# Where the small steps of a hybrid decoder layer stand between its projections: yields moved, and 6 + 10 attention tiles in place of 8 + 8

## The chip, the cores and the metric

The kernel runs on one core of one Trainium2 chip. The metric is the device time of one execution in microseconds (us). The kernel before took 2392.32 us, the median of 3 runs (2391.59 to 2392.73).

Engines: TensorE (PE; PEld is its weight load) does matmuls, VectorE (DVE) and ScalarE (ACT) work element by element and also read PSUM, GpSimd (POOL) works on SBUF, SyncE (SP) issues nearly all DMAs, one after the other.

## The reference

Two layers over one sequence of 256 positions with 2048 channels. Each layer:

```python
mod = c_act @ ada_w + ada_b                 # shift, scale, gate (2048 each)
h = rmsnorm(x, norm_w) * (1 + scale) + shift
u = h @ w_in                                # all projections in one
# branch A: gated DeltaNet, 16 heads of 128: causal conv (4 taps) + SiLU on q, k, v,
#   L2-normed q and k, decay g = -exp(a_log) * softplus(a + dt), chunked delta rule
#   (a unit lower-triangular solve in each chunk), RMSNorm per head, times SiLU(z_A)
# branch B: sliding-window (128) attention, 32 query and 4 key/value heads of 64,
#   rotary positions, a learned sink per head, times SiLU(z_B)
y = sigmoid(g_a) * (o_a @ proj_a) + sigmoid(g_b) * (o_b @ proj_b)
x = x + gate * (y @ w_out)
```

and a final RMSNorm. Everything is float32.

## The kernel before, in words

**Projections.** Activations stand transposed: 128 channels on the partitions, 256 positions along the free dimension. All weight matrices are cut into tiles of 128 output channels. `_plan` (line 46) writes out the order of the 181 tiles of a layer; the main loop (from line 946) takes them one by one. A tile is one *projection*: 16 steps over the 2048 input channels, each of two matmuls (`mm_k`, lines 291 and 292), because weights and activations are split in a high and a low part. Weights come from HBM in two halves of 512 KB (`load_half`): SP loads `win`, ScalarE casts the high part `whi` (line 203), VectorE forms the low part `wlo` (line 204). The rings: 5 `win`, 4 `whi`, 3 `wlo`. A projection's result lies in one of 2 PSUM buffers `mm` until `evac` (lines 318 and 319: ScalarE copies one half, VectorE adds the other) has put it into one of 3 buffers `ub`. The first 32 tiles of layer 0 and 8 of layer 1 are done in another way, ahead of the loop.

**Order in a layer.** After those come ba (beta and decay), kb and vb (keys and values of attention), and then two batches. A batch has 8 heads of branch A: qa 8 times, va 8 times, ka 8 times, and then 8 attention tiles, each a query and a gate projection (qb, zb) for a pair of heads. In batch 1 the second kb and vb stand between va and ka. Attention tiles 0 to 7 use the first kb and vb, 8 to 15 the second (`j = t // 8`, line 821). Then za (16), pa (16), pb (16) and wo (16), with the ga and gb that are left.

**What is done between projections.** After a projection's matmuls the loop calls `advance()`, then `run_bg(1)`, then the tile's handler. Handlers are generators: what stands behind `yield w` is issued `w` projections later than the next one's `advance()`. So `yield 0` means: behind the matmuls of the next projection; `yield 1`: behind those of the one after it. This is the order in which instructions are written; the framework then schedules them by expected readiness, with this order as priority, so an instruction may stand later than it was written, in the middle of a projection.
- `h_qa`, `h_va`, `h_ka`: convolution and SiLU of one head (`conv_silu`, from line 510: one multiply on ScalarE, three steps on VectorE at line 516, SiLU at 517). After every second head a pair is transposed on TensorE (`sumsq`, line 523, tile `sst`, with sums of squares on ScalarE at line 529; for va the transposes at line 713, tile `vtr`, scaled into `bV` at line 716).
- `h_ba`: transposes of beta and decay (`bat`), softplus as some 25 small steps on VectorE, prefix sums on TensorE (`gcp`, lines 492 and 493), a transpose (`gcr`) and a store.
- `gdn_e`: at the batch's first qa, loads the decays into `E` (1 MB broadcast), subtracts 16 times on VectorE (line 559) and takes the exponential on ScalarE (561).
- `gdn` (a background generator; every projection takes it to its next `yield`): norms, Gram matrices (`gram`, lines 613 and 614), a triangular inverse of 32-blocks in 31 small double steps on VectorE (lines 637 and 639, in five segments), a round trip through HBM, the inverse put together on TensorE (`T1p`, `Y1p`, `T2p`, `Y2p`), and the chunk steps `r`, `s1`, `ks`, `o0`, `r`, `o1`, sums of squares of the output, its norm. It begins with the last pair of ka and has 27 steps.
- `h_zb`: scores (`sc`, line 826) after the next projection, softmax on VectorE and ScalarE, transposes (`ptr`) two projections later, values (`pv`) two after those.
- `h_za` for head 8 and on needs batch 1's `gdn` to be finished: a loop runs what is left of it at once.
- Layer 0 also carries *ada* work, the modulations of gate and of layer 1: rows of 1 MB are loaded in halves into the `win` ring and multiplied and summed on VectorE (line 170). `ADA_RATE` says how many rows per projection: in layer 0 0.45 in qa and ka, 0.35 in va, 0.1 in qb and zb, 0.54 in za; in layer 1 none in these stages.

**Buffers that matter.** One buffer each: `E` (later `LX`, in which the inverse is made), `ek` (`eg` and `kdec`), `qT`, `kT`, `bV`, `GT`, `QKT`, `Y`, the rotated keys `kr`, the attention values `vnat`, the rotated query. Three: `vT` and `ub`. Two: `rot`. PSUM besides `mm`: 6 buffers for all small matmuls.

Of the kernel before, what the change touches and what calls it, by code (L numbers as in the profile page):

```python
# [25 lines left out]
HB = 8  # L26
# [19 lines left out]
def _plan(l):  # L46
    p = [("ga", i) for i in range(min(GRP[l], 16))] + [("gb", i) for i in range(GRP[l] - 16)]
    p += [("ba", 0), ("kb", 0), ("vb", 0)]
    for b in range(NB):
        for what in ("qa", "va", "ka"):  # L50
            p += [(what, b * HB + h) for h in range(HB)]
            if b == 1 and what == "va":
                p += [("kb", 1), ("vb", 1)]
        for t in range(8 * b, 8 * b + 8):
            p += [("qb", t), ("zb", t)]
    p += [("za", h) for h in range(NH)]
    for i in range(16):
        if i >= GRP[l]:
            p.append(("ga", i))
        p.append(("pa", i))  # L60
    for i in range(16):
        if i >= GRP[l] - 16:
            p.append(("gb", i))
        p.append(("pb", i))
    p += [("wo", i) for i in range(16)]
    return p
# [53 lines left out]
def build(nc):  # L120
# [11 lines left out]
    with ExitStack() as ctx:  # L132
# [26 lines left out]
        def big(name, shape, tag, dt=F32):  # L159
            return b8.tile(shape, dt, name=name, tag=tag, bufs=2 if tag == "oT" else 1)  # L160

        def gps(name, shape):
            return psg.tile(shape, F32, name=name, tag="g")
# [152 lines left out]
        def evac(ps):  # L316
            t = sm.tile([P, S], F32, name="ub", tag="ub", bufs=3)
            A.copy(t, ps[:, S:2 * S])  # L318
            V.tensor_tensor(t, t, ps[:, 0:S], op=ALU.add)  # L319
            return t  # L320
# [97 lines left out]
        for l in range(L):  # L418
# [24 lines left out]
            def cols_to_rows(cols_ap, n, name):  # L443
                pt = gps(name + "_t", [n, P])
                T.transpose(pt, cols_ap, ident)
                s = sm.tile([n, P], F32, name=name + "_s", tag="rowt", bufs=1)
                A.copy(s, pt)
                return s
# [11 lines left out]

            def h_ba(ps, i):
                u = evac(ps)
                pt = gps("bat", [P, 2, 64])
                for m in range(2):
                    T.transpose(pt[:, m, 0:48], u[0:48, m * P:(m + 1) * P], ident[0:48, 0:48])
                A.activation(beta, pt[:, :, 0:16], AF.Sigmoid)
                z = sm.tile([P, 2, NH], F32, name="spz", tag="spz", bufs=1)
                V.tensor_tensor(z, pt[:, :, 32:48],
                                pr[:, PC_DT:PC_DT + 16].unsqueeze(1).broadcast_to([P, 2, NH]), op=ALU.add)
                e = sm.tile([P, 2, NH], F32, name="spe", tag="spe", bufs=1)  # L470
                A.activation(e, z, AF.Abs)
                A.activation(e, e, AF.Exp, scale=-1.0)
                s = sm.tile([P, 2, NH], F32, name="sps", tag="sps", bufs=1)
                V.tensor_scalar(s, e, 2.0, None, op0=ALU.add)
                V.reciprocal(s, s)
                V.tensor_tensor(s, s, e, op=ALU.mult)
                s2 = sm.tile([P, 2, NH], F32, name="sps2", tag="sps2", bufs=1)
                V.tensor_tensor(s2, s, s, op=ALU.mult)
                q = sm.tile([P, 2, NH], F32, name="spq", tag="spq", bufs=1)
                V.memset(q, 1.0 / 17)  # L480
                for c in (15, 13, 11, 9, 7, 5, 3, 1):
                    V.tensor_tensor(q, q, s2, op=ALU.mult)
                    V.tensor_scalar(q, q, 1.0 / c, None, op0=ALU.add)
                V.scalar_tensor_tensor(q, q, 2.0, s, op0=ALU.mult, op1=ALU.mult)
                V.tensor_scalar(z, z, 0.0, None, op0=ALU.max)
                V.tensor_tensor(q, q, z, op=ALU.add)
                na = sm.tile([P, NH], F32, name="nega", tag="nega", bufs=1)
                A.activation(na, pr[:, PC_ALOG:PC_ALOG + 16], AF.Exp)
                V.tensor_scalar(na, na, -1.0, None, op0=ALU.mult)
                V.tensor_tensor(q, q, na.unsqueeze(1).broadcast_to([P, 2, NH]), op=ALU.mult)  # L490
                pg = gps("gcp", [P, 3, NH])
                T.matmul(pg[:, 0:2, :], tri, q, start=True, stop=True)
                T.matmul(pg[:, 2, :], ones, q[:, 0, :], start=True, stop=True)
                V.tensor_copy(gc, pg[:, 0:2, :])
                V.tensor_tensor(edec, pg[:, 2, :], gc[:, 0, :], op=ALU.subtract)
                A.activation(edec, edec, AF.Exp)
                A.activation(egc1, gc[:, 1, :], AF.Exp)
                s = cols_to_rows(gc.rearrange("p m h -> p (m h)"), 2 * NH, "gcr")
                for m in range(2):
                    dma(gc_dram[:, m, :], s[m * NH:(m + 1) * NH, :])  # L500
# [34 lines left out]
            def h_qa(ps, i):  # L535
                b, hh = divmod(i, HB)
                g = batch(b)
                if hh == 0:
                    gdn_e(b)
                    g["qT"] = big("qT", [P, HB, S], "qT")  # L540
                conv_silu(ps, i, g["qT"][:, hh, :])
                if hh % 2 == 1:
                    yield 0
                    sumsq(g["qT"], g["ssq"], hh - 1)

            def gdn_e(b):
# [16 lines left out]
            def h_ka(ps, i):  # L563
                b, hh = divmod(i, HB)
                g = batch(b)
                if hh == 0:
                    g["kT"] = big("kT", [P, HB, S], "kT")
                conv_silu(ps, 16 + i, g["kT"][:, hh, :])
                if hh % 2 == 1:
                    yield 0  # L570
                    sumsq(g["kT"], g["ssk"], hh - 1, g["kdec"])
                    if hh == HB - 1:
                        bg.append(gdn(b))

            def gdn(b):
                yield from gdn_k(b)
                yield from gdn_core(b)

            def gdn_k(b):
# [29 lines left out]
                for hh in range(HB):  # L609
                    p = gps("gram", [P, 2, 2, P])  # L610
                    for m in range(2):
                        kk = kT[:, hh, m * P:(m + 1) * P]
                        T.matmul(p[:, 0, m, :], kk, kk, start=True, stop=True)
                        T.matmul(p[:, 1, m, :], kk, qT[:, hh, m * P:(m + 1) * P], start=True, stop=True)
                    V.tensor_tensor(GT[:, hh], GT[:, hh], p[:, 0], op=ALU.mult)
                    V.tensor_tensor(QKT[:, hh], E[:, hh], p[:, 1], op=ALU.mult)
                    if hh % 3 == 2 or hh == HB - 1:
                        yield 1
                gdr = drp.tile([2 * HB, 4, 32, 32], F32, name="gdr", tag="gdr")
                for blk in range(4):  # L620
# [34 lines left out]
                for blk in range(4):  # L655
                    r = slice(32 * blk, 32 * blk + 32)
                    dma(Y[r, :, r], ydr[:, blk].rearrange("q j i -> j q i"))
                    if blk < 3:
                        d = Xa[r, :, r] if blk < 2 else Xb[r]
                        dma(d, xdr[:, blk].rearrange("q j i -> j q i"))  # L660
                yield 1
                yield 1
                GTv = GT.rearrange("p h m t -> p (h m) t")
# [34 lines left out]
            def h_va(ps, i):  # L698
                b, hh = divmod(i, HB)
                g = batch(b)  # L700
                if hh == 0:
                    g["bV"] = big("bV", [P, HB, 2, P], "bV")
                vT = sm.tile([P, S], F32, name="vT", tag="tA", bufs=3)
                conv_silu(ps, 32 + i, vT)
                if hh % 2 == 0:
                    g["vT"] = vT
                    return
                pair = (g["vT"], vT)
                yield 0
                p = gps("vtr", [P, 2, 2, P])  # L710
                for e in range(2):
                    for m in range(2):
                        T.transpose(p[:, e, m, :], pair[e][:, m * P:(m + 1) * P], ident)
                for e in range(2):
                    for m in range(2):
                        A.mul(g["bV"][:, hh - 1 + e, m, :], p[:, e, m, :], beta[:, m, i - 1 + e:i + e])

            def gdn_core(b):
# [32 lines left out]
                for h0 in range(0, HB, 4):  # L751
                    sumsq(oT, g["sso"], h0)
                    sumsq(oT, g["sso"], h0 + 2)
                    yield 1
                sso = g["sso"]
                V.tensor_scalar(g["ssq"], g["ssq"], P * EPS, P * EPS * EPS, op0=ALU.mult, op1=ALU.add)
                V.scalar_tensor_tensor(sso, sso, 1.0 / P, g["ssq"], op0=ALU.mult, op1=ALU.add)
# [305 lines left out]
```

## Time and profile before

| | |
|---|---|
| runs, median | 2392.32 us |
| the profiled execution | 2387.45 us, span of the core 2385.7 us |
| mean granted TensorE clock | 0.994 |
| busy: PE, PEld, DVE, ACT, POOL | 2298.6, 2018.0, 1792.3, 1434.1, 119.9 us |
| the loop's projections | layer 0 from 218.0 us, layer 1 from 1275.3 us |

Rows of the views have these forms. *Waits*: an engine and line, what it waited for, us in total, times, longest. *Windows*: from and to, length, busy us of PE, PEld, DVE, ACT, POOL (with instruction counts), granted clock, DMA share, GB/s. *Groups*: line, engine, operation, out<-in, shapes, count, busy us, mean ns, idle time before it and what ended it. *Timeline*: start, duration, engine, line, operation, and in brackets the idle time before it. TensorE's matmuls are pipelined: their durations overlap.

### The profile page before, as it was taken

How to read it: one execution, taken by the hardware profiler on the slowest of the kernel's cores; microseconds unless marked ns; L12 is line 12 of the kernel's file. 1: busy time of each engine (PE TensorE's matmuls, PEld its weight loads, DVE VectorE, ACT ScalarE, POOL GpSimd, SP SyncE). 2: the span in 40 equal slices, each digit the busy share in tenths (PEclk: the TensorE clock that was granted, in tenths of full speed). 3: DMA queues.
4: the chain of work that ended last, by engine and by line, in shares of the span. 5: the costliest groups of instructions: out<-in, count | busy, mean ns of one | idle time of the engine just before them, and what ended most of it. 6: DMA issues, size and time to landing. Idle time of an engine off the chain costs nothing.

```text
span 2385.7 us, 40190 instructions
## 1 busy us (share of the span) xinstructions
PE 2298.6 (96%) x14838; PEld 2018.0 (85%) x14838; DVE 1792.3 (75%) x3114; ACT 1434.1 (60%) x2691; POOL 119.9 (5%) x128
## 2 busy tenths in 40 slices
PE   7999998999999999999999999999999999999997
PEld 6999787878878887888788888888888888888886
DVE  7998887777787868888676777857678457677766
ACT  4546656777657765444455667778677665444442
POOL 0000000210002100000000001100011000000000
PEclk8999999999999999999999999999999999999999
DMA  9998667566666567999766555555555558777764
GB/s 369 353 362 283 229 227 236 158 195 199 228 234 197 178 218 259 325 308 306 221 196 213 172 182 171 159 178 174 190 169 163 172 180 269 239 244 248 248 202 144
DMA packets 192375, 536.50 MB, mean 225 GB/s; under 512 B 42737, under 2 KB 76593, under 8 KB 186545
## 3 DMA queue, kind: packets, MB, share of 16 engines
q1 hardware_dynamic: 192178, 533.93, 67.3%
q8 instruction: 117, 1.92, 0.3%
q14 instruction: 80, 0.66, 0.1%
HBM read 512.26 MB, written 16.88 MB: 222 GB/s over the span
## 4 chain that ended last, share of the span: by engine, by line
PE 65%; DVE 15%; DMA 11%; ACT 3%; issue 3%; POOL 1%; SPq 1%; DVEq 0%; ACTq 0%; POOLq 0%
PE mm L291 33%; PE mm L292 17%; DVE wlo L204 6%; DMA adaw<-ada 4%; PE mmg L253 2%; PE mmg L251 2%; PE mmg L252 2%; DMA win<-w 2%; DMA xs_dram<-x 2%; DVE LX L639 1%; DVE mt L637 1%; DMA rr<-rr_d 1%; ACT whi L203 1%; DVE cv L516 1%; DVE adaw L170 1%
## 5 line engine op out<-in xcount | busy, mean ns | idle before, releaser
L291 PE MATMUL mm<-h,whi 128*128 128x512 f32 x3616 | 1292.4, 397 | 14.4 <-DVE ub L319 14.1
L204 DVE TENSOR_TENSOR wlo<-win,whi 128x1024 fp32r<-128x1024 f32 x724 | 885.7, 1226 | 300.3 <-PE mm L292 178.5
L292 PE MATMUL mm<-h,wlo 128*128 128x256 f32 x3616 | 1025.6, 284 | 0.0
L203 ACT CAST whi<-win 128x1024 fp32r<-128x1024 f32 x724 | 755.4, 1049 | 407.1 <-PE mm L291 231.0
L291 PEld LDWEIGHTS mm<-h,whi 128*128 128x128 f32 x3616 | 681.0, 188 | 170.6 <-issue 9.2
L292 PEld LDWEIGHTS mm<-h,wlo 128*128 128x128 f32 x3616 | 681.7, 189 | 1.2 <-DVE wlo L204 0.4
L170 DVE SCALAR_TENSOR_TENSOR adaw<-adaw,cact 128x1024 f32<-128x1024 f32 x128 | 155.9, 1225 | 62.1 <-DMA adaw<-ada 61.8
L291 PE MATMUL mm<-yhl,whi 128*128 128x512 f32 x512 | 181.3, 396 | 6.6 <-DVE x L916 4.5
L291 PE MATMUL mm<-oAhl,whi 128*128 128x512 f32 x512 | 181.0, 395 | 2.2 <-DVE oAhl L324 1.8
L291 PE MATMUL mm<-oBhl,whi 128*128 128x512 f32 x512 | 180.7, 396 | 0.0
L319 DVE TENSOR_TENSOR ub<-ub,mm 128x256 f32<-128x256 f32 x290 | 120.8, 417 | 62.2 <-ACT ub L318 61.9
L516 DVE SCALAR_TENSOR_TENSOR cv<-ub,par,cv 128x253 f32<-128x253 f32 (+2 forms) x288 | 137.8, 480 | 33.7 <-ACT cv L514 30.0
L251 PE MATMUL mmg<-h,whi 128*128 128x256 f32 x512 | 140.3, 286 | 9.1 <-ACT h L376 9.1
L292 PE MATMUL mm<-oAhl,wlo 128*128 128x256 f32 x512 | 144.2, 282 | 1.9 <-DVE wlo L204 1.9
L292 PE MATMUL mm<-yhl,wlo 128*128 128x256 f32 x512 | 144.3, 282 | 0.0
L292 PE MATMUL mm<-oBhl,wlo 128*128 128x256 f32 x512 | 144.0, 281 | 0.0
L252 PE MATMUL mmg<-h,whi 128*128 128x256 f32 x512 | 143.5, 287 | 0.0
L253 PE MATMUL mmg<-h,wlo 128*128 128x256 f32 x512 | 137.4, 287 | 2.3 <-DVE wlo L204 2.2
L318 ACT COPY ub<-mm 128x256 f32<-128x256 f32 x290 | 107.1, 369 | 45.9 <-PE mm L292 44.2
L291 PEld LDWEIGHTS mm<-yhl,whi 128*128 128x128 f32 x512 | 96.1, 188 | 31.6 <-issue 7.4
L291 PEld LDWEIGHTS mm<-oAhl,whi 128*128 128x128 f32 x512 | 96.1, 188 | 25.5 <-DVE oAhl L324 2.1
L291 PEld LDWEIGHTS mm<-oBhl,whi 128*128 128x128 f32 x512 | 96.2, 188 | 22.9
(257 smaller groups left out, 2767.0 us busy)
## 6 DMA issues: line engine op xcount, KB each, us to landing
win<-w SPq DMA_DIRECT2D x724, 512.0 KB, 4.9
adaw<-ada SPq DMA_DIRECT2D x128, 512.0 KB, 5.0
adab<-ada SPq DMA_DIRECT2D x32, 1024.0 KB, 8.7
sg<-sig_dram SPq DMA_DIRECT2D x40, 128.0 KB, 2.5
rot<-ub SPq DMA_DIRECT2D x144, 32.0 KB, 2.2
sig_dram<-gacc SPq DMA_DIRECT2D x4, 1024.0 KB
E<-gc_dram SPq DMA_DIRECT2D x4, 1024.0 KB
GT<-GT_d SPq DMA_DIRECT2D x4, 1024.0 KB
```

Of the source, the lines that this page charges most:

```text
L170: V.scalar_tensor_tensor(t, t, 1.0, cact[:, hf * 1024:(hf + 1) * 1024], op0=ALU.mult, op1=ALU.mult, accum_out=acc[:, hf:hf + 1])
L203: A.copy(h, w)
L204: V.tensor_tensor(o, w, h.bitcast(F32), op=ALU.subtract)
L251: T.matmul(d, hi, m[:, 0:S], start=(k == b0 and t % 2 == 0), stop=False)
L252: T.matmul(d, hi, m[:, S:2 * S], start=False, stop=False)
L253: T.matmul(d, lo, m[:, 0:S], start=False, stop=(k == b1 - 1 and t % 2 == 1))
L291: T.matmul(ps[:, :], hi[k // 8][:, c0:c0 + P], m, start=(k == 0), stop=False)
L292: T.matmul(ps[:, S:2 * S], lo[k // 8][:, c0:c0 + P], m[:, 0:S], start=False, stop=(k == KT - 1))
L318: A.copy(t, ps[:, S:2 * S])
L319: V.tensor_tensor(t, t, ps[:, 0:S], op=ALU.add)
L516: V.scalar_tensor_tensor(y[:, j:], u[:, :S - j], w(3 - j), y[:, j:], op0=ALU.mult, op1=ALU.add)
L637: V.tensor_tensor(tv, Xt[:, 0:j + 1, j:j + 1].broadcast_to([64, j + 1, n]), Lt[:, j:j + 1, j + 1:32].broadcast_to([64, j + 1, n]), op=ALU. ...
```

## The change

`_plan` gives batch 0 attention tiles 0 to 5 and batch 1 tiles 6 to 15; the second kb and vb stay where they were, so tiles 6 and 7, which use the first ones, now come behind them. `h_ba` is cut by two more yields and its first transposes come behind one. The pairs of qa, ka and va are transposed one projection later. The background generator takes four Gram heads to a step in place of three (one step less), has four empty steps in place of two behind the inverse's DMAs, and takes the sums of squares of the output in one step in place of two: 27 steps as before. No computation is added or removed.

```diff
-        for t in range(8 * b, 8 * b + 8):
+        for t in (range(0, 6) if b == 0 else range(6, 16)):
             p += [("qb", t), ("zb", t)]
...
             def h_ba(ps, i):
                 u = evac(ps)
+                yield 0
                 pt = gps("bat", [P, 2, 64])
...
                 V.tensor_tensor(q, q, na.unsqueeze(1).broadcast_to([P, 2, NH]), op=ALU.mult)
+                yield 0
                 pg = gps("gcp", [P, 3, NH])
...
                 A.activation(egc1, gc[:, 1, :], AF.Exp)
+                yield 0
                 s = cols_to_rows(gc.rearrange("p m h -> p (m h)"), 2 * NH, "gcr")
...
                 conv_silu(ps, i, g["qT"][:, hh, :])
                 if hh % 2 == 1:
-                    yield 0
+                    yield 1
                     sumsq(g["qT"], g["ssq"], hh - 1)
...
                 conv_silu(ps, 16 + i, g["kT"][:, hh, :])
                 if hh % 2 == 1:
-                    yield 0
+                    yield 1
                     sumsq(g["kT"], g["ssk"], hh - 1, g["kdec"])
...
                     V.tensor_tensor(QKT[:, hh], E[:, hh], p[:, 1], op=ALU.mult)
-                    if hh % 3 == 2 or hh == HB - 1:
+                    if hh % 4 == 3:
                         yield 1
...
                         dma(d, xdr[:, blk].rearrange("q j i -> j q i"))
                 yield 1
                 yield 1
+                yield 1
+                yield 1
...
                 pair = (g["vT"], vT)
-                yield 0
+                yield 1
                 p = gps("vtr", [P, 2, 2, P])
...
                 for h0 in range(0, HB, 4):
                     sumsq(oT, g["sso"], h0)
                     sumsq(oT, g["sso"], h0 + 2)
-                    yield 1
+                yield 1
```

## The prediction

> **What bounds the kernel now.** I read the page first, then the waits of TensorE by layer, then matching stages of the two layers, then single places in the order of time.
>
> ```profile
> span 2385.7 us, 40190 instructions
> PE 2298.6 (96%) x14838; PEld 2018.0 (85%) x14838; DVE 1792.3 (75%) x3114; ACT 1434.1 (60%) x2691; POOL 119.9 (5%) x128
> PEclk8999999999999999999999999999999999999999
> ```
>
> TensorE is busy nearly throughout, at almost full clock. The change removes no matmul, so only idle time of TensorE inside the mixing stages can go. The waits of TensorE there, layer 0 (218 to 940 us) and then layer 1 (1275 to 1968 us); columns: total us, times, longest.
>
> ```profile
> PE sst L523 <- ACT kT L517: 9.6, 7, 2.8
> PE mm L291 <- DVE ub L319: 8.8, 6, 2.3
> PE vtr L713 <- ACT vT L517: 6.0, 5, 2.2
> ...
> PE gcp L492 <- DVE spq L490: 1.5, 1, 1.5
> PE sst L523 <- ACT qT L517: 0.7, 1, 0.7
> ```
>
> ```profile
> PE mm L291 <- DVE ub L319: 5.4, 3, 2.7
> PE gcp L492 <- DVE spq L490: 1.8, 1, 1.8
> ...
> PE vtr L713 <- ACT vT L517: 0.2, 1, 0.2
> ```
>
> The transposes of head pairs (sst of q and k, vtr of v) wait 9.6 + 6.0 + 0.7 = 16.3 us in layer 0 and 0.2 us in layer 1, for the same instructions. The stages say the same: the first three rows are va and ka of batch 0 and ka of batch 1 in layer 0, the next three their twins in layer 1 (columns: window, us, busy PE, PEld, DVE, ACT, POOL, clock, DMA).
>
> ```profile
> 289.00:340.00 51.00, 47.42 (x274) 40.96 (x273) 41.52 (x66) 29.45 (x60) 0.00 (x0) 1.00 0.70 231
> 340.00:392.00 52.00, 47.61 (x275) 41.14 (x274) 39.34 (x64) 30.07 (x71) 0.00 (x0) 1.00 0.70 229
> 651.00:703.00 52.00, 46.99 (x271) 40.62 (x270) 41.83 (x69) 28.40 (x66) 2.17 (x3) 1.00 0.73 243
> 1345.00:1391.00 46.00, 46.00 (x269) 40.44 (x268) 33.81 (x50) 29.37 (x60) 0.00 (x0) 1.00 0.55 182
> 1391.00:1438.00 47.00, 47.00 (x274) 41.09 (x273) 33.39 (x48) 30.29 (x71) 0.00 (x0) 1.00 0.57 180
> 1688.00:1735.00 47.00, 47.00 (x274) 41.14 (x273) 32.05 (x46) 28.61 (x66) 3.19 (x3) 1.00 0.57 183
> ```
>
> Eight projections take 47 us (5.9 each, transposes included) where nothing is late, and 5 us more in layer 0. What layer 0 has besides is the ada work on VectorE. The idle time of VectorE in the same three stages of layer 0 shows how it hurts (product, count, busy, mean ns, then idle before it):
>
> ```profile
> L170 DVE SCALAR_TENSOR_TENSOR adaw<-adaw,cact 128x1024 f32<-128x1024 f32 x6 | 7.3, 1223 | 3.6 <-DMA adaw<-ada 3.5
> L170 DVE SCALAR_TENSOR_TENSOR adaw<-adaw,cact 128x1024 f32<-128x1024 f32 x6 | 7.3, 1222 | 7.8 <-DMA adaw<-ada 7.8
> L170 DVE SCALAR_TENSOR_TENSOR adaw<-adaw,cact 128x1024 f32<-128x1024 f32 x8 | 9.9, 1244 | 6.8 <-DMA adaw<-ada 6.8
> ```
>
> **Part by part.** (a) *Pairs one projection later.* One place, in order of time: TensorE, then VectorE, then the start of the next projection but one.
>
> ```profile
> 370.41 0.44 PE L523 MATMUL sst<-cst,kT 128*128 128x128 f32 x2
> 373.49 0.44 PE L523 MATMUL sst<-cst,kT 128*128 128x128 f32 x2 [2.41 <-ACT kT L517]
> 376.46 1.23 DVE L170 SCALAR_TENSOR_TENSOR adaw<-adaw,cact 128x1024 f32<-128x1024 f32 x1 [2.40 <-DMA adaw<-ada]
> 377.62 0.41 DVE L319 TENSOR_TENSOR ub<-ub,mm 128x256 f32<-128x256 f32 x1
> 379.15 0.39 PE L291 MATMUL mm<-h,whi 128*128 128x512 f32 x1
> ```
>
> The first head's two transposes run, the second head's are late by 2.41 us because its convolution is. A whole projection, 5.9 us, is more than the longest such wait (2.8), so all 16.5 us can go: that is one bound. The other is VectorE. In this place the evacuation ends at 377.62 + 0.41 = 378.0; without the wait TensorE would ask for that PSUM buffer 2.41 us before 379.15, at 376.7, so 1.3 of the 2.4 us come back as an evacuation wait. By stages: VectorE's busy time plus its wait for ada is 41.5 + 3.5 = 45.0, 39.3 + 7.8 = 47.1 and 41.8 + 6.8 = 48.6 us, against 46, 47 and 47 us of TensorE. The stages can therefore shrink by at most 5.0, 4.9 and 3.4 us = 13.3, and only if VectorE waits for nothing else. I take two thirds: **-9** (0 to -16.5). The transposes move past no DMA; the start of the inverse comes one projection later, which (c) prices.
>
> [...]
>
> (b) *Decay chain in three parts.* Same instructions. The first transposes get a later earliest place (behind kb, where before they ran inside it), the prefix sums and the rows too. The prefix sums already stand behind vb, in the middle of a qa projection, where the new yields allow the same place:
>
> ```profile
> 242.86 0.41 PE L492 MATMUL gcp<-spq,cst 128*128 128x32 f32 x2 [1.55 <-DVE spq L490]
> ```
>
> So their waits of 1.5 and 1.8 us stay. **0** (-3.3 to +1); what hides the later rows is that E is first used in the gated-delta steps, stages later.
>
> (c) *Six and ten tiles.* Batch 0's inverse used to end beside tiles 6 and 7; now qa of batch 1 stands there. What was left of it from 484.4 to 505 us in layer 0:
>
> ```profile
> L639 DVE TENSOR_TENSOR LX<-LX,mt 64x247 f32<-64x247 f32 (+12 forms) x13 | 5.1, 392 | 0.1
> L637 DVE TENSOR_TENSOR mt<-LX 64x240 f32<-64x240 f32 (+11 forms) x12 | 4.1, 345 | 0.1
> L645 DVE COPY mt<-LX 64x1024 f32<-64x1024 f32 x1 | 1.6, 1597 | 0.0
> ```
>
> That is 10.8 us of VectorE. Four qa projections bring their own (rates below): 8 wlo, 12 convolution steps, 4 evacuations at 0.41, and at a rate of 0.45 about 3.6 ada halves at 1.23 plus 0.9 of wait (18.1 us over the 20 above).
>
> ```profile
> L204 DVE TENSOR_TENSOR wlo<-win,whi 128x1024 fp32r<-128x1024 f32 x724 | 885.7, 1226 | 300.3 <-PE mm L292 178.5
> L516 DVE SCALAR_TENSOR_TENSOR cv<-ub,par,cv 128x253 f32<-128x253 f32 (+2 forms) x288 | 137.8, 480 | 33.7 <-ACT cv L514 30.0
> L559 DVE SCALAR_TENSOR_TENSOR E<-E,gc,cst 128x128 f32<-128x128 f32 x64 | 17.9, 345 | 2.2 <-DMA E<-gc_dram 1.3 <-ACT ek L556 0.8
> ```
>
> 9.8 + 5.8 + 1.6 + 7.7 = 24.9 us, with the tail 35.7, beside 4 x 5.9 = 23.6 us of TensorE and the last matmuls of tiles 4 and 5. So VectorE is over by up to 12 us in layer 0; part of it waits harmlessly, since the inverse itself has four projections until its result is used (three of the four empty steps and its own). Layer 1 has no ada: 17.2 + 10.8 = 28.0. On SP the stores and reloads of the inverse and the load of E wait for the same VectorE work, weight and ada loads behind them, as they did beside tiles 6 and 7; that is inside the 12. The waits that stood beside tile 6 may go: 2.31 us (shown in (g)) and, in layer 1, (5.4 - 2.7) / 2 = 1.4. **+2** (-3.7 to +12). With 20 projections behind it, batch 1's inverse stays covered.
>
> (d) *Tiles 6 and 7 behind kb, vb of batch 1.* kr and vnat have one buffer, so batch 1's are written only when tile 7 has read the old ones. Held until then: one of three ub, one of two rot, one of six PSUM buffers. A query's ub is held from 446.60 to 455.6 us, 9.0 us, and a tile lasts two projections, 11.8 us; two buffers are enough.
>
> ```profile
> 446.60 0.37 ACT L318 COPY ub<-mm 128x256 f32<-128x256 f32 x1
> 454.85 0.74 POOL L791 TENSOR_TENSOR qr<-ub,rot 128x256 f32<-128x256 f32 x1
> ```
>
> (e) *Gram in fours, all sums of squares in one step.* The same instructions, denser: the eight extra squares with their reads are 8 x (0.29 + 0.22) = 4 us of ScalarE moved into one step. (d) and (e) together **+1** (0 to +6).
>
> ```profile
> L529 ACT ACTIVATE sq<-sst 128x128 f32<-128x128 f32 x192 | 50.3, 286 | 2.4 <-PE sst L523 2.0
> L529 ACT ACTIVATION_READ_ACCUMULATOR sq<-sst 128x1 f32 x192 | 41.6, 217 | 0.0
> ```
>
> (f) *No flush at the ninth za.* Batch 1's last two steps no longer run back to back. In layer 0 the place shows another late ada product:
>
> ```profile
> 906.88 1.23 DVE L170 SCALAR_TENSOR_TENSOR adaw<-adaw,cact 128x1024 f32<-128x1024 f32 x1 [2.59 <-DMA adaw<-ada]
> ```
>
> so little of that is the flush's: **-1** (0 to -2.6).
>
> (g) *The clock.* Two waits were followed by half clock; the one of 2.41 us was not (clock 1.00 in its stage above). The wait before tile 6's projection, then the stretches behind the two (the clock is the third column from the right):
>
> ```profile
> 484.38 0.47 PE L291 MATMUL mm<-h,whi 128*128 128x512 f32 x1 [2.31 <-DVE ub L319]
> ```
>
> ```profile
> 484.00:488.00 4.00, 3.62 (x13) 3.17 (x14) 3.45 (x11) 2.96 (x10) 0.00 (x0) 0.63 0.59 186
> 263.00:268.00 5.00, 4.87 (x19) 4.22 (x20) 3.76 (x9) 3.59 (x9) 0.00 (x0) 0.66 0.72 229
> ```
>
> They cost 5 x 0.34 = 1.7 and 4 x 0.37 = 1.5 us. With fewer long waits I count **-1** (-3.2 to +3). [...]
>
> Sum: -9 + 0 + 2 + 1 - 1 - 1 = -8 us. The profiled execution took 2387.45 us (span 2385.7), 4.9 below the median of the runs, 2392.32; I take the difference from that median: **2384 us**.
>
> **The rivals.** *The waits only move (2391).* VectorE stays the bound of layer 0's stages and the pair waits come back as evacuation waits; (a) is -2, the total -1. For it: 45.0, 47.1 and 48.6 us against 46 and 47. Against: VectorE also waits for TensorE and ScalarE now, which it need not.
>
> *Batch 0's last steps collide with batch 1's single buffers (2399).* With six tiles, gated-delta step 20 of batch 0 meets the first va of batch 1, and its last reader of bV and ek (step 24) comes behind the fifth va. Yet the first pair of new bV is due behind the fourth, so its four scalings on ScalarE wait about one projection, 5.9 us, and behind them queue weight casts and evacuations; E's exponential, its 16 subtractions (16 x 0.345 = 5.5 us of VectorE) and the sums of squares then fall together. ScalarE is at 29.4 of 46 us there without that, 2.1 free per projection: 5.9 + 4 - 2.1 = 7.8 us per layer, +15 on the forecast, 2399. It decides from 6.5 us per layer. Against it: instructions in the trace stand where inputs were expected ready, not in program order (the prefix sums above sit inside a projection), so the scalings may be placed later too. That the edit does nothing is no rival for the pairs: transposes issued behind a later projection cannot stand ahead of it.
>
> **How the numbers follow.** Forecast 0.54, waits only move 0.25, collision 0.16; 0.05 for nearly all waits going without a price (-16.5 - 2.6 - 2 = -21), 2371. The forecast's own range, (a) from -13 to -6 and (c) from 0 to +4: 2378 to 2389. 0.2% of this kernel is 4.8 us, about what a measurement can tell from no change: below 2387.5 is faster, above 2397.1 slower. Faster 0.55, same 0.27, slower 0.18. The range for 8 in 10 reaches to the collision and beyond the lucky case: 2368 to 2398.
>
> **What would show it.** Right: waits of sst and vtr in layer 0 below 2 us in total, L291's wait for ub above 8.8 but by less than 7; stages of va and ka in layer 0 at 47 to 50 us; layer 1 unchanged within 2 us. Wrong: the same stages still at 51 to 52 us (moved), or idle TensorE in va of batch 1, fourth to seventh head, in both layers (collision), or long waits in qa of batch 1 of layer 0 ((c) too small).

## The result, and the profile after

The changed kernel is slower: 2402.31 us (median of 5 runs, 2398.67 to 2406.61) beside 2392.32 us for the kernel before (5 runs, 2388.31 to 2395.84); ratio 1.0054, 95% interval 1.0034 to 1.0074. The forecast was 2384, the range 2368 to 2398. The profiled execution took 2406.61 us. First the span and granted clock, in the view by core for before and then for after:

```profile
core 0: 2385.7 us, clock 0.994
```

```profile
core 0: 2404.8 us, clock 0.986
```

The time lost to a clock below 1 is 0.006 x 2385.7 = 14.3 us before and 0.014 x 2404.8 = 33.7 us after. The difference, 19.4 us, is about as large as that of the two spans, 19.1. So, between these two executions, what some waits gained others took back, and TensorE did more of the same work at half speed. Why is read from its waits, layer 0 (218 to 950 us) and then layer 1 (1290 to 1985 us):

```profile
PE mm L291 <- DVE ub L319: 14.7, 10, 3.5
PE sc L831 <- POOL qr L796: 12.4, 5, 2.9
...
PE gcp L494 <- DVE spq L491: 0.8, 1, 0.8
...
PE sst L526 <- ACT qT L520: 0.5, 2, 0.3
```

```profile
PE sc L831 <- POOL qr L796: 9.5, 3, 4.4
PE mm L291 <- DVE ub L319: 3.7, 3, 3.1
PE gcp L494 <- DVE spq L491: 1.6, 1, 1.6
```

The waits for kT and vT, 15.6 us in layer 0, are gone. In their place stand waits of the scores for the rotated query (sc <- qr), 12.4 + 9.5 us in eight waits (before 4.4 + 1.8 in seven, the longest 1.4), and more of those for ub. The stages that the prediction watched did shrink: va and ka of batch 0 and ka of batch 1 in layer 0 (columns as in the prediction's windows):

```profile
289.00:337.00 48.00, 47.17 (x277) 41.38 (x275) 39.67 (x64) 28.86 (x64) 0.00 (x0) 1.00 0.74 239
337.00:386.00 49.00, 47.11 (x272) 40.82 (x271) 38.98 (x64) 29.35 (x67) 0.00 (x0) 1.00 0.73 243
626.00:673.00 47.00, 46.67 (x272) 40.88 (x271) 39.87 (x62) 27.26 (x60) 4.40 (x3) 1.00 0.79 262
```

48, 49 and 47 us against 51, 52 and 52. Where it was lost is seen behind the score waits and before the eighth va of batch 1 in both layers (head 7 in the code; the expectations below call it the seventh va). The windows directly behind five of the score waits, then behind the two waits at va; the clock is the third column from the right:

```profile
424.00:428.00 4.00, 4.00 (x24) 3.78 (x21) 3.98 (x14) 2.21 (x5) 0.00 (x0) 0.57 0.59 211
694.00:698.00 4.00, 3.92 (x18) 3.33 (x19) 3.12 (x13) 1.89 (x4) 0.03 (x1) 0.62 0.05 10
711.00:718.00 7.00, 6.84 (x34) 6.52 (x35) 5.42 (x15) 5.22 (x12) 1.42 (x2) 0.53 0.54 184
1482.00:1486.00 4.00, 4.00 (x23) 4.00 (x22) 3.94 (x14) 2.44 (x5) 0.00 (x0) 0.57 0.62 210
1755.00:1762.00 7.00, 5.19 (x25) 4.87 (x26) 6.32 (x14) 4.41 (x9) 2.99 (x3) 0.51 0.61 207
...
608.00:612.00 4.00, 4.00 (x17) 3.44 (x16) 2.20 (x5) 3.94 (x7) 0.00 (x0) 0.57 0.66 230
1656.00:1660.00 4.00, 3.62 (x12) 3.12 (x13) 2.82 (x5) 3.95 (x6) 0.00 (x0) 0.57 0.25 78
```

The mean is 0.57 to 0.62 over 4 us and 0.51 to 0.53 over 7, and windows of 1 us inside (425 to 426 us, 712 to 713) have 0.50: a stretch of half clock of 3.4 or 6.8 us, which costs 1.7 or 3.4 us on top of the wait.

Now the cause of a score wait. The place is the second tile of batch 0 in layer 1, before and then after, as timelines of SP, POOL and TensorE. In SP's rows the time is that of issuing.

```profile
1453.68 0.37 SPq L457 DMA_DIRECT2D GT<-GT_d  x1
1455.80 7.74 SPq L200 DMA_DIRECT2D win<-w  x3
1465.01 3.55 SPq L787 DMA_DIRECT2D rot<-ub  x4
...
1470.01 0.74 POOL L788 TENSOR_TENSOR rot<-rot,stab 128x256 f32<-128x256 f32 x1 [15.40 <-DMA rot<-ub]
...
1473.17 0.99 PE L826 MATMUL sc<-kr,qr 64*128 64x128 f32 x8 [1.43 <-POOL qr L791]
```

```profile
1468.27 0.51 SPq L792 DMA_DIRECT2D rot<-ub  x1
1468.88 0.53 SPq L457 DMA_DIRECT2D GT<-GT_d  x1
1469.46 2.83 SPq L792 DMA_DIRECT2D rot<-ub  x3
...
1476.66 1.08 POOL L793 TENSOR_TENSOR rot<-rot,stab 128x256 f32<-128x256 f32 x1 [15.15 <-DMA rot<-ub]
...
1481.12 0.92 PE L831 MATMUL sc<-kr,qr 64*128 64x128 f32 x8 [4.06 <-POOL qr L796]
```

GT is the 1 MB broadcast with which the gated-delta generator begins. Before, it was issued 11 us ahead of the four copies of the query's columns, and POOL could start 1.45 us after the last copy was issued (1465.01 + 3.55 to 1470.01). After, it is issued between the first copy and the other three, and POOL starts 4.4 us after the last (1469.46 + 2.83 to 1476.66). The generator is started by the last pair of ka; that pair comes one projection later, and so does GT. In the second tile of all four batches of the changed kernel GT stands there (issued at 411.67, 698.97, 1468.88 and 1744.12 us); the scores of these four tiles wait 2.2, 2.7, 4.1 and 4.4 us, 13.4 of the 21.9. The other four waits have no GT among their copies. The first tiles of layer 0 wait 2.9 and 2.5 us before GT is issued; with the last pair put back (below) TensorE waits 2.3 and 2.5 us for kT shortly ahead of these places instead, so there a wait seems only to have moved. So with GT issued ahead of three of the four copies POOL starts some 3 us later after the last one (4.4 against 1.45 us); the mechanism behind it is not shown.

The wait before the eighth va of batch 1 in layer 1, timelines of ScalarE, VectorE and TensorE, and the group of ScalarE's squares from 1647 to 1657 us (count, then shortest, median and longest in ns):

```profile
1646.56 1.92 ACT L564 ACTIVATE E<-E 128x2048 f32<-128x2048 f32 x1
...
1650.26 1.14 ACT L721 ACTIVATE bV<-vtr,beta 128x128 f32<-128x128 f32 x4
...
1655.30 0.48 ACT L318 COPY ub<-mm 128x256 f32<-128x256 f32 x1
...
1655.55 0.18 DVE L762 SCALAR_TENSOR_TENSOR sso<-sso,ssq 128x16 f32<-128x16 f32 x1 [3.75 <-ACT sq L532]
...
1656.38 0.76 PE L291 MATMUL mm<-h,whi 128*128 128x512 f32 x1 [3.10 <-DVE ub L319]
```

```profile
L532 ACT ACTIVATE sq<-sst x16: 292/354/384, 1651.3 to 1655.0; 128x128 f32<-128x128 f32 x16
```

ScalarE does E's exponential, two weight casts, four scalings of bV and then all sixteen squares of the one merged step, and only at 1655.30 the copy that frees TensorE's buffer.

### The profile page after: what moved, and what is told of

The parts are those of the page before. It is cut to its first block, busy times and chain, and to the rows that moved or that the text cites. A ratio compares the mean times of both kernels' runs of the same rounds, so it can differ in the third digit from the quotient of the medians.

```text
span 2404.8 us, 40159 instructions
## 1 busy us (share of the span) xinstructions
PE 2312.4 (96%) x14838; PEld 2035.7 (85%) x14838; DVE 1799.6 (75%) x3114; ACT 1442.2 (60%) x2697; POOL 128.0 (5%) x128
## 4 chain that ended last, share of the span: by engine, by line
PE 75%; DVE 10%; DMA 8%; issue 3%; ACT 2%; POOL 1%; SPq 0%; DVEq 0%; ACTq 0%; POOLq 0%
PE mm L291 38%; PE mm L292 20%; DVE wlo L204 4%; DMA adaw<-ada 3%; PE mmg L253 2%; PE mmg L251 2%; PE mmg L252 2%; DMA xs_dram<-x 2%; DMA win<-w 1%; PE sc L831 1%; DMA rot<-ub 1%; PE o L736 1%; ACT whi L203 1%; PE gram L616 1%; PE ptr L859 1%
## 5 line engine op out<-in xcount | busy, mean ns | idle before, releaser
L519 DVE SCALAR_TENSOR_TENSOR cv<-ub,par,cv 128x255 f32<-128x255 f32 (+2 forms) x288 | 138.1, 480 | 27.8 <-ACT cv L517 23.8
```

The costliest lines, as they stand in the source:

```text
L519: V.scalar_tensor_tensor(y[:, j:], u[:, :S - j], w(3 - j), y[:, j:], op0=ALU.mult, op1=ALU.add)
```

## The experiments

Two theories. **A:** the gated-delta generator starts one projection later, through the last pair of ka alone; its load then delays the rotated query, and, later on, its sums of squares fall on the end of va of batch 1. Each such wait costs itself and a stretch of half clock (1.7 or 3.4 us above). **B:** the six and ten tiles are the loss. All runs were taken beside the kernel before, whose medians in the five groups were 2388.2 to 2390.8 us; ratios are to it.

**All pairs later, nothing else** (the three `yield 0` of the diff turned into `yield 1`, in the kernel before).

> The kernel before (2392) with one part of the change, the pairs of qa, ka and va one projection later; 8 and 8 tiles, everything else as before. Theory A (the transposes gain what was forecast, some 13 us in layer 0, but the last pair of ka now starts the gated-delta generator one projection later, which puts its 1 MB load between the four loads of rotary columns of the batch's second tile: the scores wait, and waits of over 2 us are followed by half clock): -13 plus two to four such places at 3 to 5 us each: 2386 to 2396, with waits of the scores for the rotated query well above the 6.1 us of before. Theory B (the six and ten tiles are the loss, the pairs alone are only a gain): 2379, waits of the scores as before.

2406.45 us, ratio 1.0078 (1.0058 to 1.0098). The pairs alone are as slow as the whole change, and 10 us above the range that A gave: A counted 13 us of gain for the pairs, which did not come. B falls as the whole story.

**Six and ten tiles alone** (the edit in `_plan`).

> The kernel before (2392) with six and ten attention tiles behind the two batches alone. Theory A (the loss sits in the start of the attention and in the seventh va of batch 1): 2392 to 2400; a wait of TensorE at the seventh va in each layer, 3 us with half clock behind it, if the split is enough for it, none if it needs the squares in one step. Theory B (the split is the whole loss, 10 + 13 us): 2410 or more.

2400.02 us, 1.0051 (1.0031 to 1.0070). The split costs by itself too, some 12 us, at the upper end of what A allowed and less than B asked. In its trace the last va of batch 1 show no long wait (longest 1.6 us, in layer 0, before the seventh).

**All pairs later but the last of ka**, so that the generator starts where it did.

```diff
-                    yield 0
+                    yield 1 if hh < HB - 1 else 0
                     sumsq(g["kT"], g["ssk"], hh - 1, g["kdec"])
```

> The kernel before with the pairs one projection later, except the last pair of ka in each batch, which stays where it was and so leaves the start of the gated-delta generator where it was. Theory A: the gain of the pairs without the later start, 2378 to 2383, waits of the scores back at some 6 us. Theory B: the same time as with all pairs later, within 2 us.

2386.92 us, 1.0002 (0.9989 to 1.0014). One `yield` is worth 19.5 us, as A has it; but A's 2378 to 2383 was missed: the rest of the pairs gain nothing that can be measured. Its waits of TensorE in layer 0 (218 to 940 us) say why:

```profile
PE mm L291 <- DVE ub L319: 19.6, 14, 3.2
PE sc L826 <- POOL qr L791: 4.9, 4, 1.4
PE sst L523 <- ACT kT L517: 2.3, 1, 2.3
```

kT, vT and qT fell from 16.3 to 2.3 us, and ub rose from 8.8 to 19.6: 10.8 of 14.0 us came back as evacuation waits.

**The same put back in the changed kernel** (the same line there).

> The changed kernel (2402) with only the last pair of ka in each batch put back, so that the gated-delta generator begins where it did before. Theory A: the waits of the scores (21.9 us) fall to about 6, and several half-clock stretches go: 2387 to 2393. Theory B: the split stays, so 2400 to 2404.

2389.37 us, 1.0004 (0.9989 to 1.0020): 12 us better than after, level with before. A holds, and with the rest of the change in place the split no longer costs 12 us.

**Only the generator's start moved**, in the kernel before: one more `yield 1` at its beginning, pairs untouched.

> The kernel before with one thing moved: the gated-delta generator starts one projection later (the pairs stay). Theory A (the place of its 1 MB load among the rotary loads costs by itself): 2396 to 2405, the second tile's scores waiting over 2.5 us in layer 1 in both batches. Rival (it costs only because the later pairs let TensorE run ahead of VectorE): 2388 to 2393.

2413.77 us, 1.0097 (1.0082 to 1.0111): the later start costs 23 us with no other part of the change, 9 more than the most that A allowed. The second tile of layer 1 again:

```profile
1473.78 0.34 SPq L457 DMA_DIRECT2D GT<-GT_d  x1
1475.84 2.43 SPq L788 DMA_DIRECT2D rot<-ub  x4
...
1482.35 0.97 POOL L789 TENSOR_TENSOR rot<-rot,stab 128x256 f32<-128x256 f32 x1 [16.52 <-DMA rot<-ub]
...
1486.70 1.65 PE L827 MATMUL sc<-kr,qr 64*128 64x128 f32 x8 [4.33 <-POOL qr L792]
```

GT stands 2 us ahead of the copies, and POOL starts 4.1 us after the last of them. This is not the whole price: the trace also has waits for the inverse's reload (T1p <- mt, 6.5 us in three; with all pairs later 5.7 in three), which neither the kernel before nor the changed kernel has. So the 23 us are not the price of GT's place alone.

**All pairs later, and GT yet another projection later** (one more `yield 1` ahead of the load).

> The kernel before with all pairs one projection later (2406) and the 1 MB load of the gated-delta generator yet another projection later, so that it no longer falls between the loads of the rotary columns of the batch's second tile. Theory A (the place of that load is what costs): waits of 2.9 and 4.15 us of the second tile's scores gone, 2386 to 2392, as with the last pair left in place. Rival (any later start costs, because the Gram matmuls no longer stand where TensorE would wait, or the inverse ends too late): 2405 or more.

2393.71 us, 1.0016 (1.0003 to 1.0029): 13 us better than one projection later. At the second tile GT is issued behind the copies, POOL starts 1.46 us after the last (1462.90 + 2.41 to 1466.77) and the scores do not wait:

```profile
1462.90 2.41 SPq L788 DMA_DIRECT2D rot<-ub  x4
1465.43 1.81 SPq L200 DMA_DIRECT2D win<-w  x2
1467.33 0.63 SPq L455 DMA_DIRECT2D GT_d<-GT_s  x2
...
1466.77 0.74 POOL L789 TENSOR_TENSOR rot<-rot,stab 128x256 f32<-128x256 f32 x1 [10.47 <-DMA rot<-ub]
```

The waits for the inverse's reload have shrunk as well, to 0.3 us, though the generator is later still. So it is the place of its transfers among the others and not lateness as such, though the expected 2386 to 2392 was just missed: the first tile of layer 0 still waits 3.1 us.

**The changed kernel with the squares in two steps.**

```diff
                     sumsq(oT, g["sso"], h0 + 2)
-                yield 1
+                    yield 1
```

> The changed kernel (2402) with the sums of squares of the output taken in two steps again; nothing else. Theory A, second place (the sixteen reads of one step, together with E's exponential, block ScalarE and so TensorE at the seventh va of batch 1, 3.5 and 3.1 us with half clock behind each): both waits go, 5 to 10 us faster, 2392 to 2397, with the waits of the scores still at 15 us or more. Rival (the wait there comes from E and from the split, whenever the squares are taken): within 3 us of 2402, waits still there.

2397.29 us, 1.0025 (1.0008 to 1.0042). The time is just above A's range. The waits before the eighth va fall from 3.5 to 2.7 us and from 3.1 to 1.0; the score waits stay. Half of A's second place, then: without the merged step a wait remains, but a shorter one.

**Both mended** (last pair back, squares in two steps).

> The changed kernel with the last pair of ka back in its place and the sums of squares in two steps. The last pair alone gave about -13 us (2389). Theory A: the seventh va has no long wait there either, so little more, 2383 to 2390, with less half clock than the 37.5 us seen with the last pair alone. Rival (what the split costs is hidden by the spacing): back up to 2395 or more, as the split alone at 2400.

2388.36 us, 0.9993 (0.9978 to 1.0007). No further gain over the last pair alone: the merged step hurts only with the late start. It is not E's exponential alone that makes the difference: with the last pair put back and the squares merged, E's exponential also comes shortly before them (1632.3 and 1635.1 us in layer 1), but the second four scalings of bV follow them (1641.7) instead of standing ahead, and the wait before the eighth va is 0.5 us.

**Other spacing for the split** (split, Gram in fours, two more empty steps; nothing else).

> The kernel before with six and ten tiles, the Gram matrices in fours and the two further empty steps; pairs, decay chain and squares as before. The split alone took 2400. If the other spacing is what lets batch 0's inverse end beside qa of batch 1 without TensorE waiting for it: 2388 to 2393. If the split costs in any case and the later pairs made up for it: 2397 to 2402.

2396.02 us, 1.0020 (1.0008 to 1.0032), between the two expectations. The spacing seems to take back about half of what the split costs (1.0051 to 1.0020; the intervals meet at 1.0031).

**Work added in the waits** of the changed kernel:

```diff
+                if (l, t) in ((0, 0), (0, 1), (0, 6), (0, 7), (1, 1), (1, 7)):
+                    fill = gps("fill", [P, S])
+                    for _ in range(3):
+                        T.matmul(fill, ones, rot, start=True, stop=True)
                 j = t // 8
...
```

The lines left out hand `rot` from the query's handler to this place.

> The changed kernel with work added: at the six places where the scores wait for the rotated query (tiles 0, 1, 6, 7 of layer 0 and 1 and 7 of layer 1), three matmuls whose result nobody uses read the rotated columns as soon as they are there, some 3 us before the query is, so that the wait is cut in two; the order on TensorE is else the same. If half clock behind the waits is the larger part of the loss (theory A: 23.9 us of half clock behind these six in the trace, 12 us lost): 4 to 12 us faster though six times three matmuls are added, and fewer stretches of half clock there. If the waits themselves are the loss: 2402 to 2405.

2398.50 us, 1.0037 (1.0022 to 1.0051). The second tile of layer 1 and the stretch behind it:

```profile
1472.15 1.56 PE L831 MATMUL fill<-rot,ones 128*128 128x256 f32 x6 [0.65 <-POOL rot L793]
```

```profile
1475.00:1480.00 5.00, 4.52 (x41) 4.37 (x41) 5.00 (x14) 2.08 (x4) 0.43 (x1) 1.00 0.69 229
```

A wait of 4.06 us has become 0.65 + 1.76, and the clock behind it stays at 1.00, as in the windows of 4 to 7 us behind four others of the six. The time is some 4 us lower than after's, in spite of the added matmuls; the intervals overlap (next run).

**The changed kernel again.**

> The changed kernel once more, unaltered, beside the others of this group, so that the steps of some 5 us between it and the versions with the squares apart (2397) and with the added matmuls (2398.5) can be judged: 2399 to 2405 if those steps are real, 2396 to 2398 if they are within the spread of the runs.

2406.67 us, 1.0060 (1.0042 to 1.0079), a little above the upper expectation. With the first 1.0054 the steps to 1.0025 (squares apart) and 1.0037 (added matmuls) are likely real, the second one not beyond doubt.

**Work added in the waits of the mended kernel** (four places, the same kind of edit).

> The best version so far (the changed kernel with the last pair of ka put back and the squares in two steps, 2388.4) with work added: 3 matmuls whose result nobody uses stand where its trace shows TensorE waiting over 2 us in the same place run after run (layer 0: before the fifth qa and before the last head's transposes of batch 1's ka; layer 1: before the twelfth qa), and 12 short ones in the 3.8 us wait of the second pa of layer 0. Half clock behind these four places was 20.4 us in that trace. If the clock is the price of a wait: 10 us less, 2377 to 2383, below both kernels. If only the wait itself counts: 2387 to 2391.

2388.62 us, 0.9984 (0.9968 to 0.9999), no measurable gain over 0.9993. Averaged over all 12 runs the time lost to the clock (1 minus the clock, times the span, of each run) is 17 us, beside 25 without the added work, and the rest of the span is 8 us longer. So half clock is a part of the price of a wait, and these runs don't show that removing it alone returns its whole sum.

**Pairs later but the last, and four ada rows moved.** This tests why the pairs gain nothing.

```diff
-ADA_RATE = [dict(qa=0.45, ka=0.45, va=0.35, qb=0.1, zb=0.1, ...
+ADA_RATE = [dict(qa=0.45, ka=0.2, va=0.35, qb=0.225, zb=0.225, ...
```

The pairs are edited as in the version with all pairs later but the last of ka.

> The kernel before with the pairs one projection later except the last of ka (2387, no measurable gain), and four of the ada rows of layer 0 moved from the ka stages to the attention tiles (rates 0.45 to 0.2, and 0.1 to 0.225). If ada on VectorE is what turns the pairs' gain into evacuation waits: the two ka stages of layer 0 fall from 49.8 and 49.7 us to 47 to 48, the second head's wait before the first tile (2.29 us) goes, 2381 to 2385. If something else holds them: stages unchanged, or the attention tiles give it all back, 2386 to 2391.

2380.74 us, 0.9956 (0.9939 to 0.9974): below both kernels. The ka stages of layer 0, for which 47 to 48 us were expected, and the waits of layer 0:

```profile
340.00:387.00 47.00, 47.00 (x276) 41.40 (x276) 35.71 (x55) 29.89 (x68) 0.00 (x0) 1.00 0.65 212
643.00:690.00 47.00, 47.00 (x276) 41.41 (x275) 37.40 (x58) 28.21 (x62) 2.17 (x3) 1.00 0.71 234
```

```profile
PE mm L291 <- DVE ub L319: 10.1, 9, 3.1
PE sc L826 <- POOL qr L791: 4.2, 4, 1.4
PE sst L523 <- ACT kT L517: 1.9, 1, 1.9
```

TensorE never idles in them, and ub's waits are back from 19.6 to 10.1 us. The wait for kT before the first tile, which was to go, stays (1.9 us). The same kernel once more:

> The version with pairs later (except the last of ka) and four ada rows moved, once more and unaltered. If the two parts work together: 2379 to 2384, its interval against the kernel before below 0.998. If the first group of runs was lucky: 2385 to 2388, like either part alone.

2378.39 us, 0.9964 (0.9943 to 0.9984). The gain holds, some 9 us, though the interval reaches a little above the 0.998 that was asked.

**The rows moved without the pairs**, and **with everything mended**.

> The kernel before with only the four ada rows of layer 0 moved from ka to the attention tiles; pairs as before. With the pairs later as well it took 2380.7. If pairs and ada work only together: 2386 to 2391, the ka stages still waiting for kT. If the rows were the whole obstacle: 2380 to 2384, and the pairs give nothing.

2385.48 us, 0.9989 (0.9974 to 1.0004), between the two expectations. Rows alone and pairs alone (1.0002) each give nothing sure; together they give 0.9956 and 0.9964. Each gives more beside the other than alone.

> The changed kernel with the last pair of ka put back, the squares in two steps (2388.4 so far), and four ada rows of layer 0 moved from ka to the attention tiles. If VectorE's ada was what ate the pairs' gain here too: 2379 to 2384, ka stages of layer 0 at 46 to 48 us. If six and ten tiles, decay chain and spacing add something of their own: below 2378. If the denser attention stage cannot take the rows: 2386 to 2391.

2387.50 us, 0.9992 (0.9979 to 1.0006): split, decay chain and spacing add nothing to that, they take the gain away. Its ka stages do run at 47 us; it loses elsewhere, among others a score wait of 3.6 us in layer 0 (at 487.8 us).

## Why the prediction was wrong

**(a) Pairs.** The stages shrank as forecast or a little more (by 3, 3 and 5 us, forecast 9 in all; the third by more than the 3.4 us that the prediction gave as the most). The step that failed is the sentence "The transposes move past no DMA; the start of the inverse comes one projection later, which (c) prices." The last pair of ka moves the generator's first load past SP's other DMAs, into the copies of the second tile's query; (c) priced only when the inverse is needed. Its price, by the runs: 12 us in the changed kernel, or some 8 with the squares in two steps (1.0025 to 0.9993); 19.5 us (pairs with and without the last) and 23 us moved by itself, both with the waits for the inverse's reload. The prediction looked at what the moved step must finish before, not at what its own load delays.

**The rest of (a).** Even without that, the -9 did not reach the time: the pairs but the last gave 2 us (2386.92 beside 2389.13), as the rival *the waits only move* had it. Its reason was right as well (VectorE in layer 0, with ada), borne out by the rows moved. The working had the sign in hand, 1.3 of 2.4 us coming back in the one place it looked at, and weighed it less than the 5.0, 4.9 and 3.4 us by which the stages could shrink.

**(b) Decay chain.** Forecast 0; the waits of gcp are 0.8 and 1.6 us against 1.5 and 1.8. It was not run alone.

**(c) Split.** Forecast +2 (-3.7 to +12). Alone it costs 12 us, with the new spacing 5; in the mended kernel the whole change but the last pair is level with before. The bounds held it, the value taken was low.

**(d), (e).** Forecast +1 (0 to +6). The merged squares cost 7 to 8 us here (1.0054 and 1.0060 against 1.0025), above the range, and nothing that can be measured where the generator starts on time.

**(f) No flush.** Forecast -1. TensorE's idle time in za fell from 2.8 to 2.1 us in layer 0 and from 0.5 to 0 in layer 1.

**(g) Clock.** Forecast -1 (-3.2 to +3), on "fewer long waits". This is the mis-sized term: +19.4 us between the two profiled executions. The waits were fewer and longer. The prediction had seen half clock behind 2.31 us and counted on its other waits going, not on what came in their place.

The clock of every run is on record, so that the time lost to it (1 minus the clock, times the span) can be averaged over all runs of a kernel: 15 to 18 us before, 32 and 33 for the changed kernel, 23 with the last pair put back, 25 with both mended, 25 with only the generator later. So the lower clock accounts for all that the changed kernel is slower than the kernel before, but not for the whole price of the late start: moved by itself, that lengthens the rest of the span by 18 us and the loss to the clock by 7. And it tells where (a) went: in the version with both mended the rest of the span is 10 us shorter than before (2361 beside 2371), about the forecast gain, and half clock takes 8 of it back. This is an accounting; no run here shows why the waits that were left brought more half clock than those of the kernel before.

**The collision.** It named nearly the right place (va of batch 1, which it put at the fourth to the seventh head; the waits stand before the eighth) and the right work (ScalarE with the scalings, E and the squares), but not what it takes. The split alone has no long wait there, nor has the version with the last pair put back. It needs the late start: the kernel with only the pairs later, with neither the split nor the merged squares, waits 2.8 us at that place in layer 0. With wait and half clock it costs about 5 us per layer (3.5 + 1.7 and 3.1 + 1.7) against 7.8.

## What to carry to other kernels

When a step is moved, follow everything it sets off, to its first DMA, and look up what is queued there at the new time: one `yield` in front of a 1 MB load cost more (8 to 23 us here) than all the other parts gained. Where one engine carries a side job close to its limit, removing another engine's waits can just move them (here 10.8 of 14.0 us came back); move the side job in the same step and measure both together. Judge a schedule by its longest waits as well as by their sum.

## What the runs showed of the hardware

Most score waits of TensorE were followed by half clock. In the trace of the version with the squares apart the mean clock behind six of them is 0.57 to 0.60 over 4 us; the windows behind the first two:

```profile
408.00:412.00 4.00, 3.92 (x18) 3.30 (x19) 3.12 (x13) 1.89 (x4) 0.03 (x1) 0.57 0.02 7
425.00:429.00 4.00, 4.00 (x25) 3.71 (x22) 4.00 (x13) 2.19 (x4) 0.00 (x0) 0.57 0.54 192
```

In the changed kernel's own trace those of 2.0, 2.2, 2.5, 2.7, 4.1 and 4.4 us were (0.57 from 492 to 496 us behind the one of 2.0, the others in the windows above), one of 2.9 was not (1.00 from 408 to 412 us), nor were two other waits in qa of layer 0, of 2.5 and 2.1 us (1.00 from 263 to 269 and from 482 to 490 us). So the length of a wait alone does not tell whether half clock follows; what else decides it is not shown.

In layer 1 copies of 32 KB that were issued just behind a 1 MB load were awaited about 3 us longer than copies issued well before or after it (4.1 and 4.4 us from the last issue to POOL's start, against 1.45 and 1.46). Behind four weight loads of 512 KB issued straight ahead it is about as long: for the first tile of layer 0 4.0 us in the kernel before and 3.8 in the changed one, with GT still to be issued.
